# Row-scaling dispatch: smaller input and output tiles, and a third of the stores on the second DMA queue

## The chip, the cores and the metric

The kernel runs on one core of one Trainium2 chip. The metric is the device time of the run in microseconds (us); lower is better. The core's engines named here are VectorE and ScalarE, which compute, and SyncE, which only issues transfers. 16 DMA engines move data between the chip's main memory (DRAM) and the on-chip memory with its 128 partitions. Transfers are issued by SyncE or by ScalarE; the page of the profile calls SyncE's queue q1 and ScalarE's q10.

## The reference

```python
batch, seq, hidden, n_experts = 16, 1024, 512, 8      # k = 2
x_expanded = x[:, :, np.newaxis, :].repeat(k, axis=2)
weights = expert_weights[..., np.newaxis]
return (x_expanded * weights).astype(np.float32)
```

Each of 16,384 tokens is a row of 512 float32. It is written twice, once multiplied by each of its two weights. The indices of the experts are not used. 33.6 MB are read, 67.1 MB written, and little is computed.

## The kernel before

The tokens are spread over 128 partitions, so each partition has 128 tokens to handle. "A tile of T tokens" means T tokens in each partition; the tokens of a partition lie next to each other in DRAM, so a tile's row (the part of one partition) is one run of T x 2 KB in the input and T x 4 KB in the output.

*Input tiles.* Six tiles of 24, 24, 24, 24, 24 and 8 tokens (`groups`), in two buffers of 48 KB a partition (`x_pool`, `TX = 24`). `load(i)` (L82) issues a tile's load from ScalarE's queue; tile 0 is loaded in six pieces of 4 tokens (rows of 8 KB), the others in one piece. Tiles 0 and 1 are loaded at the start; `load(i + 2)` stands behind the computation of tile i, and its buffer is free only when that computation is done.

*Output tiles.* An output tile covers `TO = 12` tokens, so it has rows of 48 KB, in two buffers (`o_pool`). Each input tile of 24 gives two; the last gives one of 8 tokens. That makes 11 stores, all issued by SyncE (L115).

*Computation.* Every token and weight is one instruction on a 128x512 block: each third one a multiply on ScalarE (L100), the others `tensor_scalar` on VectorE (L106), 85 and 171 in all. They wait for the input tile, for the weights, and for the store that used the output buffer before.

*Weights.* `w_tile` holds all 256 weights of a partition. Three loads on SyncE's queue, ahead of all stores, bring it: tile 0's (L53), the next four tiles' in rows of 192 B (L54), and the last tile's (L58).

Instructions of an engine run in order, and so do the transfers of a queue on each DMA engine. A framework places the waits between engines from the buffers' use; it also gives the DMAs eight completion counters in turn, so that a DMA waits for the one eight before it, where nothing else has made sure of that.

Of the kernel before, what the change touches and what calls it, by code (L numbers as in the profile page):

```python
# [1 line left out]

# [4 lines left out]


@with_exitstack
def kernel(  # L10
    ctx: ExitStack,
    tc: tile.TileContext,
    x: bass.AP,
    expert_indices: bass.AP,
    expert_weights: bass.AP,
    out: bass.AP,
):
    nc = tc.nc

    batch, seq, hidden = x.shape  # L20
    k = expert_weights.shape[-1]
    P = nc.NUM_PARTITIONS
    ntok = batch * seq
    assert ntok % P == 0
    A_TOTAL = ntok // P

    f32 = mybir.dt.float32
    row = k * hidden
    TX = 24
    TO = 12  # L30

    groups = [[24], [24], [24], [24], [24], [8]]
    assert sum(sum(g) for g in groups) == A_TOTAL

    xf = x.rearrange("b s h -> (b s) h")
    of = out.rearrange("b s k h -> (b s) (k h)")
    wf = expert_weights.rearrange("b s k -> (b s) k")

    w_pool = ctx.enter_context(tc.tile_pool(name="w_pool", bufs=1))
    x_pool = ctx.enter_context(tc.tile_pool(name="x_pool", bufs=2))  # L40
    o_pool = ctx.enter_context(tc.tile_pool(name="o_pool", bufs=2))

    w_tile = w_pool.tile([P, A_TOTAL * k], f32)

    def rows(of_all, done, T):
        return of_all[done * P : (done + T) * P, :].rearrange(
            "(p a) n -> p (a n)", a=T
        )

    T0 = sum(groups[0])  # L50
    G = len([g for g in groups[1:] if sum(g) == T0])
    head = (1 + G) * T0
    nc.sync.dma_start(out=w_tile[:, : T0 * k], in_=rows(wf, 0, T0))  # L53
    nc.sync.dma_start(  # L54
        out=w_tile[:, T0 * k : head * k].rearrange("p (g n) -> p g n", g=G),
        in_=wf[T0 * P : head * P, :].rearrange("(g p a) n -> p g (a n)", g=G, p=P),
    )
    nc.sync.dma_start(  # L58
        out=w_tile[:, head * k :], in_=rows(wf, head, A_TOTAL - head)
    )  # L60

    tiles = []
    done = 0
    for group in groups:
        T = sum(group)
        a0 = 0
        for n in group:
            tiles.append((done, T, a0, n))
            a0 += n
        done += T  # L70

    loaded = []

    def load(i):
        if i >= len(tiles):
            return
        done, T, a0, n = tiles[i]
        x_tile = x_pool.tile([P, TX * hidden], f32)
        src = rows(xf, done, T)
        step = TX // 6 if i == 0 else n  # L80
        for at in range(0, n, step):
            nc.scalar.dma_start(  # L82
                out=x_tile[:, at * hidden : (at + step) * hidden],
                in_=src[:, (a0 + at) * hidden : (a0 + at + step) * hidden],
            )
        loaded.append(x_tile)

    for i in range(2):
        load(i)
    for i, (done, T, a0, n) in enumerate(tiles):  # L90
        x_tile = loaded[i]
        outr = rows(of, done, T)
        for t in range(n):
            if t % TO == 0:
                o_tile = o_pool.tile([P, TO * row], f32)
            for kk in range(k):
                c = (done + a0 + t) * k + kk
                o = t % TO * row + kk * hidden
                if c % 3 == 2:
                    nc.scalar.mul(  # L100
                        out=o_tile[:, o : o + hidden],
                        in_=x_tile[:, t * hidden : (t + 1) * hidden],
                        mul=w_tile[:, c : c + 1],
                    )
                    continue
                nc.vector.tensor_scalar(  # L106
                    out=o_tile[:, o : o + hidden],
                    in0=x_tile[:, t * hidden : (t + 1) * hidden],
                    scalar1=w_tile[:, c : c + 1],
                    scalar2=None,  # L110
                    op0=mybir.AluOpType.mult,
                )
            if (t + 1) % TO == 0 or t + 1 == n:
                at = t // TO * TO
                nc.sync.dma_start(  # L115
                    out=outr[:, (a0 + at) * row : (a0 + t + 1) * row],
                    in_=o_tile[:, : (t + 1 - at) * row],
                )
        load(i + 2)

# [1 line left out]
_INS = ['x', 'expert_indices', 'expert_weights']  # L122
_OUTS = [((16, 1024, 2, 512), 'float32')]


# [23 lines left out]
```

## Time and profile before

| | |
|---|---|
| median of 3 runs | 240.6 us (240.56 to 240.91) |
| profiled execution: span from first to last instruction | 238.9 us |
| VectorE busy, ScalarE busy | 69.0 us, 54.9 us |
| DMA moved | 100.81 MB, mean 422 GB/s over the span |
| first and last store issued | 13.4 us, 218.4 us |

The span is what the profile shows of one execution; the time of a run is somewhat longer. "Busy" counts only an engine's own instructions. The DMA line of the page divides the span into 40 slices and gives the busy share of the 16 DMA engines in tenths.

The page's list of transfers (what, queue, count, size of each, median us from issue to landing):

```profile
out_dram<-o_tile SPq DMA_DIRECT2D x10, 6144.0 KB, 33.6
x_tile<-in_x_dram ACTq DMA_DIRECT2D x4, 6144.0 KB, 43.9
x_tile<-in_x_dram ACTq DMA_DIRECT2D x6, 1024.0 KB, 10.6
out_dram<-o_tile SPq DMA_DIRECT2D x1, 4096.0 KB, 19.5
x_tile<-in_x_dram ACTq DMA_DIRECT2D x1, 2048.0 KB, 24.0
w_tile<-in_expert_weights_dram SPq DMA_DIRECT2D x1, 96.0 KB, 11.1
```

"ACTq" is ScalarE's queue and "SPq" SyncE's. A load of 6 MB takes 43.9 us from issue to landing, because it shares the engines with the stores.

### The profile page before, as it was taken

The page shows a single profiled execution, that of the slowest core. Times are in us where ns is not written, and L with a number is a line of the kernel's source. Part 1 is how long each engine was busy: PE and PEld are TensorE (multiplying, and loading weights), DVE is VectorE, ACT ScalarE, POOL GpSimd, SP SyncE. Part 2 cuts the span into 40 slices and gives each one's busy share as a digit, 9 for nine tenths or more (in the row PEclk, how much of TensorE's full clock was granted, in tenths as well). Part 3 has the DMA queues.
Part 4 walks back from the last instruction along what each step waited for, and adds up shares of the span by engine and source line. Part 5 has one row for each costly group of instructions (what it writes and reads, how often), then busy time and mean ns, then how long its engine had stood idle before and what let it go on. Part 6 is the DMA issues. An engine that isn't in the chain of part 4 may idle for free.

```text
span 238.9 us, 364 instructions
## 1 busy us (share of the span) xinstructions
DVE 69.0 (29%) x171; ACT 54.9 (23%) x86; POOL 0.2 (0%) x4
## 2 busy tenths in 40 slices
DVE  0890300004609100190063037003706406415000
ACT  0870300004308000170071034003406106213000
POOL 0000000000000000000000000000000000000000
DMA  6999999999999999999999999999989899999994
GB/s 244 420 443 395 495 395 395 494 428 395 428 494 395 413 494 411 395 446 469 403 411 502 395 420 453 436 411 428 469 379 496 381 428 469 436 411 428 436 439 197
DMA packets 3986, 100.81 MB, mean 422 GB/s; under 512 B 1168, under 2 KB 1168, under 8 KB 1168
## 3 DMA queue, kind: packets, MB, share of 16 engines
q1 hardware_dynamic: 2400, 67.24, 65.2%
q10 hardware_dynamic: 1584, 33.56, 33.1%
q14 instruction: 2, 0.02, 0.0%
HBM read 33.69 MB, written 67.11 MB: 422 GB/s over the span
## 4 chain that ended last, share of the span: by engine, by line
DMA 66%; DVE 13%; another core or an unknown queue 11%; issue 0%; DVEq 0%; SPq 0%
DMA out_dram<-o_tile 54%; DVE o_tile L106 13%; DMA x_tile<-in_x_dram 11%; DVEq L144 0%; DVEq L106 0%; SPq L115 0%
## 5 line engine op out<-in xcount | busy, mean ns | idle before, releaser
L106 DVE TENSOR_SCALAR o_tile<-x_tile,w_tile 128x512 f32<-128x512 f32 x171 | 69.0, 480 | 149.3 <-DMA out_dram<-o_tile 105.3
L100 ACT ACTIVATE o_tile<-x_tile,w_tile 128x512 f32<-128x512 f32 x85 | 53.6, 709 | 155.5 <-DMA out_dram<-o_tile 116.8
L100 ACT ACT_TABLE_LOAD x1 | 1.3, 1283 | 6.7 <-DMA x_tile<-in_x_dram 6.7
L133 POOL MEMSET const-bfloat16-1.0<- 128x1 bf16 x1 | 0.1, 101 | 0.0
L133 POOL MEMSET const-uint8-127<- 128x1 uint8 x1 | 0.1, 101 | 0.0
L133 POOL MEMSET const-float32-0.0<- 128x1 f32 x1 | 0.1, 98 | 0.2 <-issue 0.2
L133 POOL MEMSET const-float32-1.0<- 128x1 f32 x1 | 0.1, 98 | 0.0
## 6 DMA issues: line engine op xcount, KB each, us to landing
out_dram<-o_tile SPq DMA_DIRECT2D x10, 6144.0 KB, 33.6
x_tile<-in_x_dram ACTq DMA_DIRECT2D x4, 6144.0 KB, 43.9
x_tile<-in_x_dram ACTq DMA_DIRECT2D x6, 1024.0 KB, 10.6
out_dram<-o_tile SPq DMA_DIRECT2D x1, 4096.0 KB, 19.5
x_tile<-in_x_dram ACTq DMA_DIRECT2D x1, 2048.0 KB, 24.0
w_tile<-in_expert_weights_dram SPq DMA_DIRECT2D x1, 96.0 KB, 11.1
w_tile<-in_expert_weights_dram SPq DMA_DIRECT2D x1, 24.0 KB, 2.9
w_tile<-in_expert_weights_dram SPq DMA_DIRECT2D x1, 8.0 KB, 13.2
```

The costliest lines, as they stand in the source:

```text
L100: nc.scalar.mul(out=o_tile[:, o : o + hidden], in_=x_tile[:, t * hidden : (t + 1) * hidden], mul=w_tile[:, c : c + 1],)
L106: nc.vector.tensor_scalar(out=o_tile[:, o : o + hidden], in0=x_tile[:, t * hidden : (t + 1) * hidden], scalar1=w_tile[:, c : c + 1], scala ...
L133: nc = _bacc.Bacc("TRN2", target_bir_lowering=False, num_devices=1)
```

## The change

Input tiles become eight of 16 tokens (rows of 32 KB, two buffers), output tiles sixteen of 8 tokens (rows of 32 KB, four buffers). The on-chip memory used is the same, 192 KB a partition for the two pools. Tile 0 is loaded in four pieces of 4 tokens. The weights come in two loads: tile 0's, and all others' in rows of 128 B, 7 for each partition.

The first output tile (j = 0) is computed as before, with 11 instructions on VectorE and 5 on ScalarE. For each later one, VectorE makes the first four tokens (`CH = 4`) in one `tensor_tensor` product of 128x4096, in which the input is repeated over the two weights and each weight over its 512 elements, and ScalarE makes the other four tokens in eight multiplies of 128x512.

Of the sixteen stores, j = 3, 7, 11, 13 and 15 are issued by ScalarE, in the queue of the input loads; the other eleven stay with SyncE. `behind()` fixes the order on ScalarE: its instructions stay behind the DMA that was issued last there.

```diff
-    TX = 24
-    TO = 12
+    TX = 16
+    TO = 8
+    XB = 2
+    OB = 4
+    CH = 4
-    groups = [[24], [24], [24], [24], [24], [8]]
+    groups = [[16]] * 8
...
-    o_pool = ctx.enter_context(tc.tile_pool(name="o_pool", bufs=2))
+    o_pool = ctx.enter_context(tc.tile_pool(name="o_pool", bufs=OB))
...
     nc.sync.dma_start(out=w_tile[:, : T0 * k], in_=rows(wf, 0, T0))
     nc.sync.dma_start(
-        out=w_tile[:, T0 * k : head * k].rearrange("p (g n) -> p g n", g=G),
-        in_=wf[T0 * P : head * P, :].rearrange("(g p a) n -> p g (a n)", g=G, p=P),
-    )
-    nc.sync.dma_start(
-        out=w_tile[:, head * k :], in_=rows(wf, head, A_TOTAL - head)
+        out=w_tile[:, T0 * k :].rearrange("p (g n) -> p g n", g=G),
+        in_=wf[T0 * P :, :].rearrange("(g p a) n -> p g (a n)", g=G, p=P),
     )
...
+    def behind():
+        return tc.issue_after(issued[-1].ins) if issued else ExitStack()
...
-        step = TX // 6 if i == 0 else n
+        steps = [4, 4, 4, 4] if i == 0 else [n]
...
+    S = A_TOTAL // TO
+    beside = [j for j in range(S) if j % 4 == 3 or j == S - 3]
...
+                for kk in range(k if j == 0 or t >= CH else 0):
+                    if j > 0 or c % 3 == 2:
+                        with behind():
+                            nc.scalar.mul(
...
+            if j > 0:
+                c = (done + a0 + at) * k
+                nc.vector.tensor_tensor(
+                    out=o_tile[:, : CH * row].rearrange(
+                        "p (t k h) -> p t k h", t=CH, k=k
+                    ),
+                    in0=x_tile[:, at * hidden : (at + CH) * hidden]
+                    .rearrange("p (t h) -> p t h", t=CH)
+                    .unsqueeze(2)
+                    .to_broadcast([P, CH, k, hidden]),
+                    in1=w_tile[:, c : c + CH * k]
+                    .rearrange("p (t k) -> p t k", t=CH)
+                    .unsqueeze(3)
+                    .to_broadcast([P, CH, k, hidden]),
+                    op=mybir.AluOpType.mult,
+                )
+            dst = outr[:, (a0 + at) * row : (a0 + at + TO) * row]
+            if j in beside:
+                with behind():
+                    issued.append(nc.scalar.dma_start(out=dst, in_=o_tile))
+            else:
+                nc.sync.dma_start(out=dst, in_=o_tile)
+        load(i + XB)
```

## The prediction

> **What bounds the kernel now.** I read the page's busy shares, then its slices of DMA, then DMA by stage (windows), then the chain of waits in order of time, and last the single DMA packets of the trace: one packet is one partition's row, moved by one of 16 DMA engines.
>
> ```profile
> span 238.9 us, 364 instructions
> ...
> DVE 69.0 (29%) x171; ACT 54.9 (23%) x86; POOL 0.2 (0%) x4
> ...
> DMA  6999999999999999999999999999989899999994
> ...
> q1 hardware_dynamic: 2400, 67.24, 65.2%
> q10 hardware_dynamic: 1584, 33.56, 33.1%
> ```
>
> q1 is the SyncE queue (weights, stores), q10 the ScalarE queue (loads). VectorE and ScalarE are busy for under a third; the DMA engines are full in all slices but the first and the last. The windows (stretch; its length; VectorE, ScalarE, GpSimd busy; clock; DMA share; GB/s) say where they are not:
>
> ```profile
> 0.00:18.00 18.00, 10.80 (x27) 9.47 (x14) 0.20 (x4) 1.00 0.97 373
> 18.00:113.00 95.00, 21.68 (x54) 17.19 (x28) 0.00 (x0) 1.00 1.00 431
> ...
> 128.00:235.00 107.00, 30.14 (x75) 23.21 (x37) 0.00 (x0) 1.00 1.00 430
> 235.00:239.00 4.00, 0.00 (x0) 0.00 (x0) 0.00 (x0) 1.00 0.23 98
> ```
>
> From 18 to 235 us the engines move 430 GB/s with no hole; whatever is lost is lost before 18 and after 235. The chain of waits (start, length, what) says the same in another form:
>
> ```profile
> 141.29 6.44 DVE o_tile L106 x16
> ...
> 147.78 33.46 DMA out_dram<-o_tile
> ...
> 181.36 6.43 DVE o_tile L106 x16
> ...
> 187.85 25.96 DMA out_dram<-o_tile
> ```
>
> Compute of 6.4 us alternates with stores of 26 to 33 us; the stores take that long because other transfers stand ahead of them or share the engines, so shortening the 6.4 us gains nothing while another transfer is queued.
>
> **The single packets.** A row of 48 KB takes 1.815 us, one of 32 KB 1.213, of 16 KB 0.611, of 8 KB 0.310: 9 ns a packet and 27.2 GB/s. Per engine that is 112 x 1.815 + 8 x 1.213 + 8 x 0.611 + 48 x 0.310 = 232.8 us of data, with weights (40 x 0.015 + 8 x 0.011) and completions (25 x 0.009) 233.7. The engines end at 236.4 on average, so 2.7 us are lost: 2.3 to 2.5 until the first rows flow at full pace (first packet at 1.84, its first rows 0.4 to 1.0 us each), and 0.7 between 15.4 and 18 us, where the last 8 KB rows of tile 0 take up to 0.66 us, just as the first store joins them; 0.3 is what the fit is off. After 18 us the loss does not grow by 0.1 us, whether loads and stores mix or stores run alone. The last engine ends at 237.6 (1.2 us behind the mean), the span 1.3 us later at 238.9, and the median of the runs, 240.6, lies 1.7 us above the span; I keep these 1.3 and 1.7.
>
> **The change, part by part.**
>
> *Rows of 32 KB.* After: 128 store rows and 56 load rows of 32 KB, 32 of 8 KB: 184 x 1.213 + 32 x 0.310 = 233.1, +0.3 us. Weights: 64 rows of 128 B, about 0.0135 us each between the measured 0.015 (192 B) and 0.011 (64 B): 0.86 against 0.69, +0.2. Four more completions: nothing. Together **+0.5**. The 32 KB price was seen on 128 store rows only; a load row could differ, but at 48 KB and 8 KB loads follow the same fit, so I take it.
>
> *Fewer, larger VectorE instructions; half of the work on ScalarE.* VectorE goes from 171 scalar multiplies to 11, and 15 products of 128x4096. No such product is in the trace: eight scalar multiplies (spaced 6.42/16 = 0.40 us) bound it below at 3.2 us, the same at half the rate above at 6.4; I take 4.5, since it reads a second full operand. ScalarE makes 8 multiplies a store, 5.01 us in the timeline, 125 in all. A tile of 8 tokens is thus ready in 5.0 to 6.4 us where its store alone needs 8 x 1.213 = 9.7. Cost nothing, hidden under the stores queued; with that cover gone, up to 6.4 us once for each store so exposed. [...]
>
> *Buffers.* Two of 48 KB become two input and four output buffers of 32 KB, the same SBUF. From a store's landing to its successor's first packet pass 5.0 to 6.4 us of compute and 1.1 us (load at 0.73, packet at 1.84) to 3.6 us (first store, issued 13.38, packet at 16.97): 10 us at most, while up to three other stores (9.7 us each alone, more when shared) are waiting. No hole.
>
> *Stores on the ScalarE queue.* Five DMA issues of 0.36 us go into ScalarE's order, 1.8 us, hidden by its idle 150 us. Each waits for VectorE's product of the same tile; behind it on ScalarE stand the next input load and the next eight multiplies. With 4.5 us against ScalarE's own 5.0 the wait is nothing, at 6.4 it is 1.4 us (twice that where two products follow each other), and the load queued behind it is not needed for another 20 us. A load now lies behind a 4 MB store in its ring: it lands 10 to 19 us later. The tightest place is the end: when the last input lands at about 200 us, stores 12 and 13 still hold some 19 us of work against 10 at most for store 14. The order of instructions shows one wait more: a DMA waits for the one eight before it in program order, whose completion counter it shares (store 8 for store 3, the last input load for store 6); each of these lands 20 us or more before it is asked for, so nothing. Total bytes are unchanged, and one ring alone already fills the engines (194 to 235 us), so this part is worth nothing.
>
> *Weights and the first store.* Weight rows go one for one with load rows: 192 B and 64 B rows last from 5.5 to 14.4 us beside 8 KB rows, except for 240 of them (15 an engine) that pass at 5.0 to 5.5, between two loads. The second weight load now has 56 rows an engine: 15 so, 24 beside what is left of tile 0 (ends near 12.9), 8 beside tile 1 (to 22.5), 8 beside tile 2 (issued near 13.8 + 5.0 = 18.8, so before tile 1 ends; to 32.2). The first store, issued near 11, is queued on SyncE's ring behind them and starts near 32 instead of 13. What is late next: tile 1's compute, which needs those weights, starts near 33. What covers it: three input tiles keep the engines full until 32, and stores 0 and 1, by then issued, for 19.4 us more, when store 2 (33 + 5 = 38) is long there. Cost: nothing. [...]
>
> *The loss of 0.7 us at the first store.* Two readings: 8 KB rows suffer beside a store (later joins, of 48 KB loads to running stores at 30, 78, 128 us, lose under 0.1), and with the first store after the 8 KB rows it is gone, -0.7; or the first store costs this wherever it is, 0. The rows speak for neither alone; I take the middle, **-0.35**.
>
> *The ends.* Spread of the engines at the end, 1.2 us: single rows that took up to 0.65 us too long (14 rows of 48 KB, all while loads and stores mixed) make it. It may come out between 0.5 and 2; I leave it.
>
> Sum: 238.9 + 0.5 - 0.35 = 239.1 us of span, with 1.7 **240.8 us**. Differences under 0.2% (0.5 us) are about what a measurement of this kernel can tell from none, so the forecast is no change.
>
> **Rivals.**
>
> *First-store loss comes back in full, slower.* Place: the start of store 0. Price: the 0.7 us stay, +0.5 from shorter rows is not paid back: 241.1 to 241.2; it decides if the rows around the first store are again slower than 1.213 or 0.310. For it: first loads too were slow when they began (0.4 to 1.0 us for 0.31). Against: later joins cost nothing.
>
> *Row starts at powers of two, slower.* Store rows lie 64 KB apart instead of 96, load rows 32 instead of 48. If one store row in ten takes the mean excess of the 14 slow ones (0.25 us), 128 x 0.1 x 0.25 = 3.2 us: 244. Against: the last store (32 KB apart) had no row over 1.216. [...]
>
> *Loss gone and an even finish, faster.* -0.7 at the first store, and loads that mix with stores for less long (the first three input tiles run alone) leave fewer slow rows, so the last engine is 0.6 instead of 1.2 us behind: 238.9 + 0.5 - 0.7 - 0.6 = 238.1, 239.8. For it: all 14 slow rows fell in mixed stretches.
>
> *The change does not do what it says:* stores beside the loads cannot raise a rate that is full; this is contained in the forecast.
>
> **How the numbers follow.** No change 0.45 (240.2 to 241.1 alone); first-store loss back, with an uneven finish up to 242, 0.28; powers of two, or a ring run dry near the end, 0.08; faster 0.19. The range 239.8 to 242.0 leaves out the 0.08 and about half of the 0.19. Faster 0.19, same 0.45, slower 0.36.
>
> **What would show it.** DMA full from 3 to 235 us; q1 and q10 nearer to each other (46 and 54 MB); the second weight load landing after 30 us; 32 KB rows of 1.213 us in loads too; VectorE products of 3.2 to 6.4 us. Wrong if a slice in the middle falls below 9, if 32 KB rows differ by direction, or if the engines' mean end moves by over 1 us.

## The result, and the profile after

The changed kernel takes 251.15 us at the median of 4 runs (248.06 to 255.04), the kernel before 240.62 (240.56 to 240.91). The ratio is 1.035, 95% interval 1.030 to 1.039; it leaves out the two slowest runs (252.18 and 255.04 us) and so lies below the ratio of the medians, 1.044. The changed kernel is slower by 3 to 4%, and its runs differ by 7 us, where those of the kernel before differ by 0.4.

The page of the changed kernel, the lines that answer to those shown of before:

```profile
span 248.3 us, 274 instructions
...
DVE 70.5 (28%) x26; ACT 79.2 (32%) x126; POOL 0.2 (0%) x4
...
DMA  7999999999999999999999999999999999959992
...
q10 hardware_dynamic: 2304, 54.53, 52.6%
q1 hardware_dynamic: 2640, 46.27, 43.8%
...
L131 DVE TENSOR_TENSOR o_tile<-x_tile,w_tile 128x4096 f32<-128x4096 f32 x15 | 65.9, 4423 | 150.5 <-DMA x_tile<-in_x_dram 146.7
...
x_tile<-in_x_dram ACTq DMA_DIRECT2D x7, 4096.0 KB, 50.7
...
w_tile<-in_expert_weights_dram SPq DMA_DIRECT2D x1, 112.0 KB, 23.0
```

The bytes are split between the queues as planned, the engines compute for under a third of the time, and the DMA engines look full. Two things are new: a "5" in slice 36, and stretches in which the engines are full and move less. The windows (stretch; length; busy times of the engines; clock; DMA share; GB/s) show both:

```profile
20.00:70.00 50.00, 17.61 (x4) 19.94 (x32) 0.00 (x0) 1.00 1.00 428
70.00:80.00 10.00, 0.00 (x0) 0.00 (x0) 0.00 (x0) 1.00 1.00 394
80.00:130.00 50.00, 17.61 (x4) 19.93 (x32) 0.00 (x0) 1.00 1.00 430
130.00:140.00 10.00, 0.00 (x0) 0.00 (x0) 0.00 (x0) 1.00 0.98 377
...
190.00:196.00 6.00, 0.00 (x0) 0.00 (x0) 0.00 (x0) 1.00 1.01 366
196.00:219.00 23.00, 0.52 (x1) 0.69 (x2) 0.00 (x0) 1.00 1.00 430
219.00:225.00 6.00, 6.00 (x2) 6.00 (x11) 0.00 (x0) 1.00 0.44 191
```

At 70 to 80, 130 to 140 and 190 to 196 us a share of 0.98 to 1.01 goes with 366 to 394 GB/s: rows are under way all the time, and take longer (those of 32 KB up to 2.2, 2.7 and 2.6 us for 1.213). At 219 to 225 the share itself is 0.44: over half of the engines' time passes with nothing to move. The timeline (start, length, what, idle before it and what ended it) says what the transfers waited for:

```profile
218.31 9.91 ACT L116 ACTIVATE o_tile<-x_tile,w_tile 128x512 f32<-128x512 f32 x16 [31.18 <-DMA x_tile<-in_x_dram]
218.48 8.76 DVE L131 TENSOR_TENSOR o_tile<-x_tile,w_tile 128x4096 f32<-128x4096 f32 x2 [32.45 <-DMA x_tile<-in_x_dram]
223.35 0.33 SPq L150 DMA_DIRECT2D out_dram<-o_tile  x1
```

The last input tile lands at 218 us. The stores that were queued run out between 219 and 223, and store 14 can't be issued before 223.35.

**Why so late.** The traces have 16 completion packets of 4 bytes for each of the 29 transfers, one behind each DMA engine's part, and these show when it was done. For the last input tile they lie between 208.5 and 211.2 us on 15 engines, and at 217.9 on the sixteenth; ScalarE, which waits for the tile, begins at 218.31, so the last engine decides. For the second weight load they lie anywhere between 11.1 and 23.9 us. In the kernel before, the last engine was never more than 2.3 us behind the median one. I call this distance the spread. What one queue has waiting on one engine I call a ring; the transfers of both queues, 13 of SyncE's and 16 of ScalarE's in this trace, have 16 such packets each, so I count one ring of either queue on each engine.

**Where the time went.** From the single packets the span can be taken apart. "Data" is the time of all packets of an engine at 9 ns each and 27.2 GB/s; "lost" is the time that has passed less the data moved by then, averaged over the engines; "last" is how far the last engine ends behind that average; 1.3 us follow.

| kernel | median of runs | span | data | lost to 20 us | lost 20 to 210 | lost after 210 | last |
|---|---|---|---|---|---|---|---|
| before | 240.6 | 238.9 | 233.7 | 2.9 | -0.1 | -0.1 | 1.2 |
| after | 251.2 | 248.3 | 234.3 | 2.8 | 3.7 | 3.2 | 3.0 |
| e1_all_sync | 245.0 | 243.5 | 234.3 | 2.8 | 1.9 | -0.1 | 3.3 |
| e8_beside_late | 243.6 | 241.2 | 234.3 | 2.6 | 1.7 | -0.1 | 1.4 |
| e10_load_first | 248.0 | 246.8 | 234.3 | 2.6 | 3.1 | -0.1 | 5.5 |
| e9_weights_beside | 244.9 | 243.1 | 234.3 | 2.6 | 2.4 | -0.1 | 2.5 |
| e5_weights_scalar | 242.7 | 241.2 | 234.3 | 2.6 | 1.4 | -0.1 | 1.7 |

The 9.4 us between the two spans are 0.6 of data, 3.8 of slow rows between 20 and 210 us (176 of the 2851 rows from 20 us on were over 30 ns late, 4.1 us an engine; 14 of 2020 and 0.2 us before), 3.3 of the dry stretch at 219 to 225 us, 1.8 of the last engine. Of the 4.1 us, 3.0 belong to rows that began at 70 to 80, 130 to 140 and 190 to 200 us. There, in ScalarE's ring, an input load follows a store.

### The profile page after: what moved, and what is told of

Read it like the earlier page. It is cut to its first block, busy times and chain, and to the rows that moved or that the text cites. A ratio compares the mean times of both kernels' runs of the same rounds, so it can differ in the third digit from the quotient of the medians.

```text
span 248.3 us, 274 instructions
## 1 busy us (share of the span) xinstructions
DVE 70.5 (28%) x26; ACT 79.2 (32%) x126; POOL 0.2 (0%) x4
## 4 chain that ended last, share of the span: by engine, by line
DMA 56%; another core or an unknown queue 20%; ACT 13%; DVE 2%; ACTq 1%; issue 0%
DMA out_dram<-o_tile 32%; DMA x_tile<-in_x_dram 24%; ACT o_tile L116 13%; DVE o_tile L131 2%; ACTq L89 0%; ACTq L116 0%
## 5 line engine op out<-in xcount | busy, mean ns | idle before, releaser
L116 ACT ACTIVATE o_tile<-x_tile,w_tile 128x512 f32<-128x512 f32 x125 | 77.9, 708 | 144.7 <-DMA x_tile<-in_x_dram 142.1
L131 DVE TENSOR_TENSOR o_tile<-x_tile,w_tile 128x4096 f32<-128x4096 f32 x15 | 65.9, 4423 | 150.5 <-DMA x_tile<-in_x_dram 146.7
L122 DVE TENSOR_SCALAR o_tile<-x_tile,w_tile 128x512 f32<-128x512 f32 x11 | 4.5, 481 | 6.3 <-DMA x_tile<-in_x_dram 6.3
```

Source lines behind the costliest of these rows:

```text
L116: nc.scalar.mul(out=o_tile[:, o : o + hidden], in_=x_in, mul=w_tile[:, c : c + 1],)
L122: nc.vector.tensor_scalar(out=o_tile[:, o : o + hidden], in0=x_in, scalar1=w_tile[:, c : c + 1], scalar2=None, op0=mybir.AluOpType.mult,)
L131: nc.vector.tensor_tensor(out=o_tile[:, : CH * row].rearrange("p (t k h) -> p t k h", t=CH, k=k), in0=x_tile[:, at * hidden : (at + CH) * ...
```

## The experiments

Ratios are to the kernel before, with 95% intervals. Where one is missing, the runs lay too far apart for one.

**e1_all_sync: no store on ScalarE's queue.**

```diff
-    beside = [j for j in range(S) if j % 4 == 3 or j == S - 3]
+    beside = []
```

> The changed kernel with all sixteen stores on SyncE's queue. Theory 'order' (a store ahead of a load in the ScalarE ring makes the last input land late, at 218 us, and the rings run dry for 3 us): the last input lands before 200 us, no hole near 221, 241 to 244 us. Theory 'switch' (loads that follow a store in the same ring start with slow rows, 0.7 to 1.0 us a time): these losses near 72, 132, 193 us go as well, 241 to 242. Theory 'spacing' (row starts at powers of two make rows slow): the slow rows stay, wherever loads begin; only the hole may go, 244 to 248.

244.97 us (242.59 to 245.83), ratio 1.016 (1.011 to 1.022). The dry stretch is gone, and so is half of the loss between 20 and 210 us. The windows at the three places:

```profile
70.00:80.00 10.00, 0.22 (x1) 0.38 (x1) 0.00 (x0) 1.00 0.99 413
130.00:140.00 10.00, 3.53 (x2) 4.05 (x8) 0.00 (x0) 1.00 1.00 429
190.00:196.00 6.00, 1.73 (x1) 1.76 (x3) 0.00 (x0) 1.00 1.01 437
```

The stores beside the loads cost 6.2 us of the medians, 1.9% by the ratios; 4.4 us of the medians remain that they don't explain.

**e2_space48 and e4_space128: other distances between rows.**

```diff
-    groups = [[16]] * 8
+    groups = [[16, 16, 16], [16, 16, 16], [16, 16]]   # e2
+    groups = [[16] * 8]                               # e4
```

The weights come in one load for tile 0 and one for the rest of each group.

> The changed kernel, with the tokens grouped 48, 48, 32 a partition instead of 16, so that rows of 32 KB lie 96 KB (input) and 192 KB (output) apart, in the last group 64 and 128; the weights come in four loads with longer rows. 'Spacing': the loss by slow rows between 35 and 200 us (3.7 us on the mean of the engines) falls below 1, and with it the lag of the slowest engine; 242 to 246. 'Switch' and 'order': slow rows and hole as in the changed kernel, 248 to 254. 'Uneven weights' (the 56 small weight rows of an engine put the engines out of step): fewer weight rows, 24 an engine, so the spread of landings is smaller; 242 to 250.

> The changed kernel with all 128 tokens of a partition in one group: rows lie 256 KB (input) and 512 KB (output) apart, powers of two again, four to eight times as far; weights in two loads, 16 rows an engine. 'Spacing': at least as many slow rows as in the changed kernel, 248 us or more. 'Switch' and 'order': as the changed kernel, 248 to 254. 'Uneven weights': better, 242 to 248.

e2: 251.17 us (245.24 to 255.58), no ratio; its four runs lie 10 us apart, so its time says little. e4: 249.62 us (248.60 to 253.64), ratio 1.036 (1.032 to 1.040), as slow as the changed kernel. Row distances that are no powers of two in the first two groups (e2), and powers four and eight times as large (e4), leave the slow rows as they were in the profiled runs: 4.0 and 4.1 us an engine, most of it in the same three places, and a dry stretch. With as many slow rows where the distances are no powers of two, spacing falls as their cause. That the larger distances of e4 cost nothing isn't shown by itself, since its weight rows changed with them. In both the first stores land with a spread of 0.4 us, but tile 1 with 1.3 us in e2 and 2.3 in e4. With stores ahead of loads in the ring the spread grows from there: the last input tile lands with 9.1 and 7.7 us.

**e3_before_beside: the kernel before, three stores on ScalarE's queue.**

```diff
+                q = nc.scalar if j in (2, 5, 8) else nc.sync
-                nc.sync.dma_start(
+                q.dma_start(
```

> The kernel before, with stores 2, 5 and 8 of its eleven on ScalarE's queue, nothing else changed. 'Switch': a loss of about 0.8 us at each load behind such a store, 242 to 243.5. 'Order': last input later, perhaps a dry ring near the end, 240.6 to 246. 'Spacing': no slow rows (rows 48 and 96 KB apart), 240.4 to 241.5.

244.41 us (242.14 to 246.92), ratio 1.012 (1.007 to 1.017). It is slower with 48 KB rows and two buffers too. But the 0.8 us "at each load behind such a store" are not there: in its profile, of the slowest of the four runs, only 0.6 us are lost between 20 and 210 us, 2.0 after, and the last engine is 4.6 behind. So "switch" falls for rows of 48 KB; what the stores on this queue bring here is the spread, up to 10.8 us. For rows of 32 KB it doesn't fall: in all five profiles with stores among the loads (the changed kernel, e2, e4, and e9 and e10 below) the slow rows gather where a load follows a store, 0.4 to 1.1 us an engine each time.

**e8_beside_late and e10_load_first: does it matter that loads stand behind stores?** e8 leaves only stores 13 and 15 on ScalarE's queue. e10 leaves all five, and issues the next input load ahead of the store.

```diff
+    beside = [13, 15]                       # e8
...
+            if at + TO == n and j in beside:    # e10
+                load(i + XB)
             if j in beside:
```

> The changed kernel with only stores 13 and 15 on ScalarE's queue, behind which no input load stands. 'Order' (loads behind stores in the ring are what costs): as e1, 243 to 246, the last input lands before 200 us. If stores on that queue cost by themselves, whatever is behind them: 246 to 251.

> The changed kernel, all five stores on ScalarE's queue, but the next input load is issued ahead of the store instead of behind it. 'Order' (a load behind a store in the ring is what costs): the last input lands before 200 us, no hole near 221, 243 to 246. If what costs is the number of stores on that queue, or the two queues' equal shares: 248 to 254.

e8: 243.64 us (243.00 to 246.03), ratio 1.014 (1.008 to 1.019): stores with no load behind them cost nothing over e1. e10: 248.04 us (245.59 to 255.38), ratio 1.024 (1.020 to 1.028). In e10 there is no dry stretch, as "order" had it; a line of its windows:

```profile
219.00:225.00 6.00, 2.30 (x1) 2.79 (x5) 0.00 (x0) 1.00 1.00 431
```

That is worth 3.1 us of the medians (1.1% by the ratios), near the 3.3 of the account. But the time lies in the other range, and the rest of the cost stays: spread 8 to 9 us, slow rows 3.5 us an engine, the last engine 5.5 us behind. The slow places have moved with the order; tile 4's load now follows store 3, and tile 6's store 7:

```profile
90.00:100.00 10.00, 4.43 (x1) 5.02 (x8) 0.00 (x0) 1.00 0.98 390
150.00:160.00 10.00, 2.59 (x1) 2.69 (x5) 0.00 (x0) 1.00 0.99 383
```

So, between these two kernels, the order of store and load decides whether rings run dry (a share of 0.44 against 1.00 at 219 to 225 us), and the slow rows stay in both orders (4.1 and 3.5 us an engine), as does the spread (up to 10 and 8 to 9 us).

**e5_weights_scalar and e9_weights_beside: the small weight rows out of the way.** The second weight load goes to ScalarE's queue between tile 0 and tile 1, where its 56 rows an engine pass in one go (it lands 10.9 us after its issue in e5 and 10.8 in e9, against 23.0 in the changed kernel); e5 has all stores on SyncE, e9 the five on ScalarE.

```diff
     for i in range(XB):
         load(i)
+        if i == 0:
+            with behind():
+                issued.append(nc.scalar.dma_start(out=w_tile[:, T0 * k :]...
```

> The kernel of e1_all_sync (all stores on SyncE), and the second weight load moved to ScalarE's queue between the pieces of tile 0 and tile 1, so that its 56 small rows an engine pass in one go and the first store is not behind them. 'Uneven weights' (the 16 engines let the weight rows pass at different times, 11 to 24 us, and stay out of step): landings within 2 us of each other, 240.5 to 242. 'Depth' (four output buffers let the engines drift apart, however they start): spread grows again later, 243 to 246 as e1.

> The changed kernel with its second weight load on ScalarE's queue between tile 0 and tile 1, as in e5_weights_scalar, the five stores still on ScalarE's queue. If uneven weights and stores ahead of loads cost separately (2.2 and 6.2 us by the runs so far): 248 to 250, engines in step at first and out of step after the first store that stands ahead of a load (44 us). If the stores cost only because the engines start out of step: 242 to 244.

e5: 242.74 us (242.21 to 243.36), ratio 1.008 (1.006 to 1.011). e9: 244.86 us (244.17 to 244.99), ratio 1.017 (1.015 to 1.019). The first stores now land with a spread of 0.2 to 0.3 us. With the bytes, the tiles and the stores all as in the changed kernel, moving this one load takes 6.3 us of the medians away (1.8% by the ratios), and the runs of e9 lie within 0.8 us of each other. Both times lie between the two ranges that I had given. A line of e9's timeline, and three of its windows:

```profile
211.87 9.91 ACT L120 ACTIVATE o_tile<-x_tile,w_tile 128x512 f32<-128x512 f32 x16 [30.27 <-DMA x_tile<-in_x_dram]
```

```profile
130.00:140.00 10.00, 0.00 (x0) 0.00 (x0) 0.00 (x0) 1.00 0.99 393
190.00:196.00 6.00, 0.00 (x0) 0.00 (x0) 0.00 (x0) 1.00 1.02 377
219.00:225.00 6.00, 1.80 (x1) 2.78 (x5) 0.00 (x0) 1.00 1.01 437
```

The last input lands 6.4 us earlier than in the changed kernel, and nothing runs dry, though the loads still stand behind stores. The slow rows behind the stores are still there, 393 and 377 GB/s. The four kernels together:

| medians, us | weights on SyncE | weights on ScalarE |
|---|---|---|
| all stores on SyncE | 245.0 (e1) | 242.7 (e5) |
| five stores on ScalarE | 251.2 (after) | 244.9 (e9) |

By the medians each part alone costs 2.1 to 2.3 us and both together 8.4; by the ratios it is 0.8% each and 2.7% together. Either way the two cost more together than apart. My reading is that the one puts the engines out of step and the other turns that into late inputs. It is argued from the landings and not shown whole: in e4 the weights hold up no store and the first stores land together, and yet it is as slow as the changed kernel. One engine was 2.3 us behind there at tile 1; whether that, or the other row distances, makes e4 slower than e9 was not tried.

**e6_two_out and e14_step_two_out: two output buffers,** in e1 and in e5 (`OB = 2`).

> The kernel of e1_all_sync with two output buffers instead of four, so less is queued. 'Depth': engines that run ahead find nothing to do and wait for the last, the spread stays below 3 us, as in the kernel before; 240.5 to 243. 'Uneven weights': the spread of 9 to 11 us at the first stores now leaves engines without work early: 244 to 250.

> The kernel of e5_weights_scalar (all stores on SyncE, weights in one go, 242.7) with two output buffers instead of four. 'Depth' (four buffers let engines drift apart): spread below 1.5 us throughout, 241 to 242. If two buffers cost by themselves, as e6_two_out suggested, by leaving engines without work: 243.5 to 247.

246.04 us (1.021, 1.018 to 1.023) and 245.54 us (1.017, 1.013 to 1.021): neither is faster than with four. e14 is slower than e5; e6 isn't clearly slower than e1, whose interval reaches 1.022. The spread falls at first (0.2 us at 52 us in e6) and returns to 4 and 5. So two buffers don't keep the engines together, and "depth" falls.

**e7_before_out8 and e11_rows16: shorter store rows.** e7 is the kernel before with `TO = 8` and three output buffers; e11 is e5 with `TO = 4`, `CH = 2` and eight.

> The kernel before with output tiles of 8 tokens in three buffers instead of 12 in two; all else, loads, weights and computation, as before. 'Depth': one more store queued, the spread of landings grows above 3 us, 241.5 to 244. 'Uneven weights': in step as before, 240.3 to 241.5 (shorter rows cost 0.2).

> The kernel of e5_weights_scalar (242.7) with output tiles of 4 tokens in eight buffers: store rows of 16 KB, 32 stores. By the 9 ns a packet it costs 1.1 us more: 243.5 to 244.5. 'Rows' (shorter store rows bring slow rows, beyond the 9 ns, as e7_before_out8 hints): 245 to 250.

e7: 243.52 us (241.34 to 244.35), ratio 1.013 (1.008 to 1.017). e11: 242.92 us (240.82 to 243.43), ratio 1.007 (1.005 to 1.010). Rows half as long are no slower than e5's, beyond their packets (+1.3 us of data) even faster, with a spread of 0.2 to 1.9 us from 48 us on. So it isn't row length as such. The profiled run of e7, in step to 0.9 us from 189 us on, took 241.3 us; the median is 243.5, and why its runs differ I can't say.

**e12_before_weights, e13_before_rows_double, e15_before_pieces: the kernel before, only its start changed.** e12 moves the second and third weight load to ScalarE's queue; e13 cuts the second in two of half the row length; e15 loads tile 0 in pieces of 4, 4, 4 and 12 tokens.

> The kernel before with its second and third weight loads on ScalarE's queue, behind the pieces of tile 0. The 0.7 us lost when the first store joins the 8 KB rows was gone in e5_weights_scalar. If the small weight rows beside the loads are its cause: 239.8 to 240.2, faster than both kernels. If the first store costs it anyway: 240.4 to 240.8.

> The kernel before with its second weight load cut into two of half the row length, so that 64 instead of 32 small rows an engine stand ahead of the first store; bytes, tiles, buffers and stores unchanged. 'Out of step' (small rows that pass at a different pace on each of the 16 engines put the engines out of step, and that costs time): spread of landings above 5 us at the first stores, 242.5 to 245. 'Row size and buffers' (the cost belongs to 32 KB rows or four buffers): 240.5 to 241.2, since 32 rows more cost 0.4 us.

> The kernel before with tile 0 loaded in pieces of 4, 4, 4 and 12 tokens instead of six of 4: 24 KB rows where the last 8 KB rows stood beside the first store. If the 0.7 us lost there belongs to the 8 KB rows: 239.7 to 240.2. If the first store costs it anyway: 240.4 to 240.8. If the weight rows, now beside longer rows, put the engines out of step: 242 to 245.

e12: 244.78 us (241.70 to 245.94), ratio 1.013 (1.009 to 1.018); here the same move that helped e5 puts the engines 18.5 us apart (store 1 lands at 48 us on the median engine and at 66.5 on the last), and the last one ends 3.7 behind the mean. My hope for the 0.7 us at the first store failed. e13: 243.95 us (242.51 to 245.65), ratio 1.014 (1.009 to 1.018). Its small rows last until 33.2 us; its windows:

```profile
30.00:33.00 3.00, 0.00 (x0) 0.00 (x0) 0.00 (x0) 1.00 0.63 264
33.00:36.00 3.00, 0.00 (x0) 0.00 (x0) 0.00 (x0) 1.00 0.87 263
36.00:40.00 4.00, 0.00 (x0) 0.00 (x0) 0.00 (x0) 1.00 0.87 283
```

The engines run dry one after the other, and then all are slow for 5 us. It isn't as clean as I meant it: the extra DMA shifted the completion counters (the traces have eight, for 25 transfers in the kernel before; there the first store shares one with the second weight load, which has landed by 12.3 us). Tile 1's load was issued at 12.1 us instead of 6.2, and the first store, whose tile was computed by 23.7 us, waited for a weight load whose counter it shares and was issued at 33.8. The line of SyncE's waits:

```profile
SPq L121 <- DMA w_tile<-in_expert_weights_dram: 30.7, 1, 30.7
```

So e13 doesn't show what small rows cost by themselves. e15: 241.75 us (240.45 to 252.78), ratio 1.002 (1.000 to 1.004); six of twelve runs take 240.5 to 241.2 us, one 242.3 and five 250.7 to 252.8, with nothing changed but the length of a few rows at the start. In the profiled run, which took 240.6 us, the first store lands with a spread of 8.2 us and the second with 1.1: there the engines were out of step at first, and it cost nothing. No run at 251 us was profiled, so what makes those slow isn't known.

None of these kernels beats the one before.

## Why the prediction was wrong

The forecast was 240.8 us, no change. By its own steps:

- *Rows of 32 KB, +0.5.* Right: 234.3 against 233.7 us of data, and load rows cost what store rows do, 1.213 us, where nothing disturbs them.
- *VectorE's product, 4.5 us.* Right: 4.42 in the page, hidden, as was ScalarE's share.
- *The first-store loss, -0.35.* Not paid: 2.8 us were lost by 20 us, against 2.9. e8 and e10, which start like the changed kernel, lost 2.6, as did e5, and e12 lost 3.4; the cause stays open.
- *Weights and the first store, "cost: nothing".* This is one of the two steps that failed. I reckoned with one engine as if it stood for all 16, and so with one time, 32 us, for the weights. They were through on the first engine at 11.1 us and on the last at 23.9. Of the 896 rows 454 passed by 5.5 us, 28 an engine and not 15, and store 0's first rows began at 14.9 us, not 32. On average the engines had work (a DMA share of 1.00 from 20 to 210 us); but from then on they were at different places in their rings. That this load costs is shown by e9 against the changed kernel, 6.3 us of the medians; that it costs by the engines being out of step is argued.
- *Stores on the ScalarE queue, "worth nothing", and "no hole".* The second step. That the SyncE queue alone fills the engines is right (before, from 194 to 235 us, a share of 1.00 and 431 GB/s), and some lateness of the last input was covered, by 19 us of work against 10: but its landing is that of the slowest engine, 218 us and not 200 (the other 15 were done at 208.5 to 211.2), and the work left is that of the faster ones, which had none. That is 3.3 us. The rows of a load behind a store, which I had put at 1.213 us, were slow too, 3.0 us an engine at the three places. In all these stores cost 6.2 us of the medians, 1.9% by the ratios (e1).
- *The ends, "between 0.5 and 2; I leave it".* 3.0 at the end, and a spread of up to 10 on the way. I had seen the spread and taken it for a matter of the last microsecond.
- *Slow rows.* The rival of powers of two gave 244 us and the right sign; its mechanism is refuted by e2, where distances that are no powers of two have as many slow rows. In e4, whose store rows lie 512 KB apart, their median is 1.213 us, as in the changed kernel. The slow rows are real, 4.1 us an engine. They were fewer in e5 (1.9 us), in e11 (1.2) and before (0.2), where the spread was small for most of the run; but e9, with a spread of at most 4.1 us up to 195 us, has 2.8, more than e1 with 2.4 and a spread of up to 11. So the spread alone doesn't make them. What the four kernels with the most (3.5 to 4.1 us: the changed one, e2, e4, e10) have in common is loads behind stores in one ring.

What stays open: what makes a row slow, behind a store and elsewhere; how much of the cost of the weight load is that of engines out of step; and 1.5 us that e5 loses between 20 and 210 us beyond the kernel before.

## What to carry to other kernels

Where transfers are the bound, look at when each of the 16 engines completes its part, not only at the mean share: the last input tile of the changed kernel landed with its last engine, at 217.9 us, when the other 15 had been done by 211.2, and a full DMA line (a share of 1.00 from 20 to 210 us) did not show that the engines were up to 10 us apart. Be wary of many small rows on a queue in front of large ones while the other queue carries large rows: each engine let the 56 of the changed kernel pass at its own pace, and they were through at 11.1 to 23.9 us, where the 40 of the kernel before were through at 12.1 to 14.4. And don't queue stores among the loads that the next compute needs (6.2 us of the medians in the changed kernel, by e1): the average cover may be ample (here 19 us of work against 10), and the slowest engine's is not.

## What I had not expected

Rows that began together were slow once, and once not. In e13, when all rings had run dry, the 16 engines began a 48 KB store row within 0.15 us of each other (34.65 to 34.80 us): the rows took 2.3 to 2.9 us instead of 1.815, and the load rows behind them 1.9 to 3.6. In the changed kernel 15 engines began store 14 within 0.15 us of each other after the dry stretch (224.18 to 224.32 us), and their rows of 32 KB took 1.22 us, next to the 1.213 of an undisturbed one. So beginning together is not enough, and what slowed the rows of e13 is open. In the changed kernel, the loads that follow a store in ScalarE's ring begin slowly (1.2 to 2.2 us for 1.213 at 73 to 77 us, up to 2.7 at 130 to 140), those that follow a load much less so: at 34 to 40, 90 to 102 and 150 to 162 us the median load row takes 1.213 to 1.218 us and none over 1.68. And a start that differs only in the length of a few rows made one kernel (e15) finish at 241 us or at 251; the cause of that isn't shown.
